# Sums of the down weights made on VectorE from tiles already loaded, stored from GpSimd's queue

## The chip, the cores and the metric

The kernel runs on one core of a Trainium2 chip. The metric is the device time of one execution in microseconds (us). An execution is timed apart from the profile; the profile is one execution of its own.

## The reference, cut to what matters

Two sequences (512 and 1024 tokens of width 1024, float32) each pass through one layer: a mixer (dilated attention beside gated linear attention) and then a feed-forward part. The change touches the feed-forward part alone:

```python
def swiglu(hn, w_gate, w_up, w_down):
    return (jax.nn.silu(hn @ w_gate) * (hn @ w_up)) @ w_down
x = x + swiglu(rmsnorm(x, norm2_g[l]), w_gate[l], w_up[l], w_down[l])
return rmsnorm(x, final_norm_g)
```

`w_gate` and `w_up` are 1024 x 2816, `w_down` is 2816 x 1024.

## The kernel before, in words

The mixer comes first and is not touched. The feed-forward part then takes the 1536 tokens in two blocks of 768 (`NT` = 6 tiles of 128 tokens). Within a block it goes through 11 groups (`NG`) of 2 x 128 columns of `w_gate` and `w_up`, and 2 x 128 rows of `w_down`.

Every product is made of float32 operands that are split in a high part (ScalarE copy, L96) and a low part (VectorE subtraction, L97), and takes three passes of TensorE. The products with `w_gate` and `w_up` go by a scheme of seven products of half-size matrices in place of eight (Strassen in Winograd's form). On the weights' side it needs, of the four quarters of a weight matrix, four sums named 1 to 4; on the tokens' side the forms b11, m2, b21, t3, m1, t4, b22. A product of one form is 12 matmuls of 384 columns (L1116).

- **First block.** The raw quarters of `w_gate` and `w_up` are loaded by SyncE (SP) into tiles `wr` (six buffers, L1032, one 256 KB transfer each, L1065). VectorE makes the sums (`summed`, L1069 to L1082, and L1098) and SP stores them to DRAM (L1073, L1100). After each group comes `down` (L1195): `w_down`'s four quarter tiles are loaded (L1061), split (`rows`, L1188), and each token tile takes 12 matmuls of 512 columns into `dn`, which VectorE adds to the accumulator (L1207). It needs no sums of `w_down`.
- **Second block.** The sums are loaded ready-made (L1063, L1061). `w_down` goes by the scheme of seven too, over pairs of groups (`down` at L1216, matmuls at L1228); only the last group is plain.
- **Strips.** The sums of `w_down` that the second block needs are made between DRAM places while the first block runs: `strips` (L66 to L79) lists 32 copies from ScalarE's queue (L73) and 32 accumulating transfers from GpSimd's queue (L74), 352 KB each. The main loop gives them out at an even pace, each tied to the end of a product (L1342 to L1350).
- **Turns.** In groups 3, 5 and 7 of the first block the tokens of the second block are prepared: `rows` (L934) loads two token tiles into `hx` (L937), with a sum of squares on ScalarE (L940) and the power on GpSimd (L91), at products 0 and 3 of `w_gate`; `turn` (L951) then transposes them (L960), makes the forms, splits them into tiles of the pool `wc`, which the split weights use too, and stores them from SP (L968) in pieces of 512 bytes.

Order of the work. The list `units` (L1260 to L1279) holds the products in order. A plan says at which unit which weight is prepared: four products ahead (`AHEAD`, L1260), `rows` of `w_down` at products 3 to 6 of `w_up` (L1304). Loads are taken from the list `wanted` in order, as far ahead as the count `room` (6, L1311) allows; a prepared tile gives its place back (L1102, L1193). From this the framework makes the queues of the engines, in an order of its own near to the program's, with all waits; every engine and every queue works in order. Pools give a buffer out again when all its readers and stores are done. The pool `sm` (four buffers) holds sums 1 and 2 of a weight in the first block, and two intermediate tiles of a turn.

Of the kernel before, what the change touches and what calls it, by code (L numbers as in the profile page):

```python
# [18 lines left out]
P = 128  # L19
# [24 lines left out]
def tile_trunk(ctx: ExitStack, tc: tile.TileContext, a: dict):  # L44
# [12 lines left out]
    quarters, sums, bulk = {}, {}, []  # L57
    for wn in ("w_gate", "w_up"):
        quarters[wn] = {(i, j): a[wn][0][512 * j:512 * j + 512, FH * i:FH * i + FH] for i in range(2) for j in range(2)}
        sums[wn] = {n: dram.tile([NF // 2, P, 512], F32, name=f"{wn}s{n}") for n in (1, 2, 3, 4)}  # L60
    quarters["w_down"] = {
        (i, j): a["w_down"][0][FH * i:FH * i + FH, 512 * j:512 * j + 512] for i in range(2) for j in range(2)
    }
    sums["w_down"] = {n: dram.tile([FH, 512], F32, name=f"w_downs{n}") for n in (1, 2, 3, 4)}

    def strips():  # L66

        sm, qu = sums["w_down"], quarters["w_down"]
        n, step = 8, FH // 8
        out = [[] for _ in range(n + 3)]  # L70
        for c in range(n):
            rows = slice(step * c, step * c + step)
            copy = lambda o, i, r=rows: nc.scalar.dma_start(out=o[r], in_=i[r])  # L73
            add = lambda o, i, r=rows: nc.gpsimd.dma_start(out=o[r], in_=i[r], accum_op=ALU.add, max_dma_last_dim=2048)  # L74
            out[c] += [(copy, sm[x], qu[y]) for x, y in ((1, (0, 0)), (3, (0, 1)), (2, (1, 1)), (4, (1, 0)))]
            out[c + 1] += [(add, sm[1], qu[0, 1]), (add, sm[3], qu[1, 1])]
            out[c + 2] += [(add, sm[2], sm[1])]
            out[c + 3] += [(add, sm[4], sm[2])]
        return [x for y in out for x in y]  # L79
# [820 lines left out]
    if True:  # L900
# [131 lines left out]
        wr_p = pool(left, "wr", 6, side="left")  # L1032
# [3 lines left out]
        e_p = pool(left, "e", 15, side="left")  # L1036
# [8 lines left out]
        RIGHT = ((0, 0), 2, 3, 4, 1, (1, 1), (1, 0))  # L1045

        class Group:
# [7 lines left out]
            def raw(self, wn, x, n=0):  # L1055

                lo = self.grp * P
                own, tag = (sm_p, "sm") if self.blk and n % 3 == 2 else (wr_p, "wr")
                t = own.tile([P, 512], F32, tag=tag, name=f"r{wn}{self.blk}{self.grp}_{n}")
                if wn == "w_down":  # L1060
                    nc.sync.dma_start(out=t, in_=(sums[wn][x] if isinstance(x, int) else quarters[wn][x])[lo:lo + P])  # L1061
                elif isinstance(x, int):
                    nc.sync.dma_start(out=t, in_=sums[wn][x][self.grp])  # L1063
                else:
# [4 lines left out]
            def summed(self, wn, n):  # L1069

                q = lambda i, j: self.r[wn, (i, j)]
                add = lambda o, i0, i1: nc.vector.tensor_tensor(out=o, in0=i0, in1=i1, op=ALU.add)
                put = lambda x: nc.sync.dma_start(out=sums[wn][x][self.grp], in_=self.r[wn, x])  # L1073
                if n == 1:
                    for x in (1, 2):
                        self.r[wn, x] = sm_p.tile([P, 512], F32, tag="sm", name=f"s{x}{wn}{self.grp}")
                    add(self.r[wn, 1], q(1, 0), q(1, 1))
                    add(self.r[wn, 2], self.r[wn, 1], q(0, 0))
                    add(q(1, 0), q(0, 0), q(1, 0))
                    self.r[wn, 3] = q(1, 0)  # L1080
                    for x in (1, 2, 3):
                        put(x)  # L1082

            def prepare(self, wn, n):

                nm = f"c{wn}{self.blk}{self.grp}_{n}"
                x = (RIGHT if wn == "w_down" else LEFT)[n]
                if wn == "w_down":
                    wc = wd_p.tile([P, 2, 512], F32R, tag="wd", name=nm)
                else:  # L1090
                    own, tag = (hx_p, "hx") if n in (2, 5) else (wc_p, "wc")
                    wc = own.tile([P, 2, 512], F32R, tag=tag, name=nm)
                    if not self.blk:
                        self.summed(wn, n)
# [12 lines left out]
            def product(self, wn, n):  # L1107

                x = FORMS[n]
                if n in (0, 1, 3, 4):  # L1110
                    self.ps[n] = gu_p.tile([P, 512], F32, tag="gu", name="gu")[:, 0:H]
                own = {2: 0, 5: 3, 6: 4}.get(n, n)
                ps, wc, (xh, xl) = self.ps[own], self.w.pop((wn, n)), self.b.B[x]
                for k in range(KH):
                    for i, (wp, src) in enumerate(((0, xh), (0, xl), (1, xh))):
                        ins = nc.tensor.matmul(ps, wc[:, wp, k], src[:, k], start=(own == n and k == 0 and i == 0),  # L1116
                                               stop=(k == KH - 1 and i == 2), skip_group_check=True)
                getattr(self, wn)(n, ps)
                return getattr(ins, "ins", ins)
# [50 lines left out]
            def left(self, n):  # L1170

                sub = lambda o, i0, i1: nc.vector.tensor_tensor(out=o, in0=i0, in1=i1, op=ALU.subtract)
                neg = lambda o, i0, i1: nc.vector.scalar_tensor_tensor(
                    out=o, in0=i0, scalar=-1.0, in1=i1, op0=ALU.mult, op1=ALU.subtract
                )
                a11, a12, a21, a22 = [self.e[x] for x in ((0, 0), (1, 0), (0, 1), (1, 1))]
                if n == 1:
                    self.s1, self.s2 = self.tmp("s1"), self.tmp("s2")
                    sub(self.s1, a22, a21)
                    neg(self.s2, self.s1, a11)  # L1180
                elif n == 2:
                    sub(a21, a11, a21)
                elif n == 5:
                    neg(self.s2, self.s2, a12)
                src = a11 if n == 0 else self.s2 if n in (1, 5) else (a21, a22, self.s1)[n - 2] if n < 5 else a12
                self.w["left", n] = self.factor(f"f{n}_", src)

            def rows(self, f, c):  # L1188
# [3 lines left out]
                split(self.wd[f, c][:, 0], self.wd[f, c][:, 1], self.r["w_down", (f, c)])  # L1192
                return 1  # L1193
# [22 lines left out]
        def down(blk, grps, n, q):  # L1216
# [3 lines left out]
            fresh = n in (0, 4, 6)  # L1220
# [4 lines left out]
            for i, g in enumerate(gs):  # L1225
                x, w = g.w["left", n], g.w["w_down", n]
                for m, (xp, wp) in enumerate(((0, 0), (0, 1), (1, 0))):
# [3 lines left out]
                        (1, 1, ALU.subtract), (0, 1, ALU.subtract), (0, 0, ALU.add))[n]  # L1231
# [57 lines left out]
        def plan(i, key, wn, n):  # L1289
            todo.append((i, key, wn, n))  # L1290
            if wn == "rows":
                wanted.append((key, "w_down", n, 0))
            elif key[0]:
# [4 lines left out]
        for i, u in enumerate(units):  # L1298
            if u[0] == "p":
# [4 lines left out]
                if u[2] == "w_up" and groups[u[1]].plain and u[3] > 2:  # L1304
                    plan(i, u[1], "rows", divmod(u[3] - 3, 2))
# [5 lines left out]
        room = 6  # L1311

        def prepare_to(i):
            nonlocal room
            while todo and todo[0][0] <= i:
# [6 lines left out]
                if wn == "rows":  # L1322
                    room += g.rows(*n)
                else:
                    room += g.prepare(wn, n)
                    if wn == "w_down":
                        g.left(n)
# [4 lines left out]
        strip = strips()  # L1332
        total = len(strip)
        for i, u in enumerate(units):
            prepare_to(i)
            if u[0] == "p":
# [3 lines left out]
                ins = groups[key].product(wn, n)  # L1340

                if key[0] == 0 and 0 < key[1] < NG - 1:  # L1342
                    at = 14 * (key[1] - 1) + n + (7 if wn == "w_up" else 0) + 1
                    while strip and (total - len(strip)) * 14 * (NG - 2) < at * total:
                        f, o, x = strip.pop(0)
                        x = f(o, x)
                        tc.add_manual_dep(
                            getattr(x, "ins", x), ins.name,
                            mybir.DependencyInfo(mybir.DependencyClass.Sync, mybir.DependencyReason.DATA), reason="pace",
                        )  # L1350
# [82 lines left out]
```

## Time and profile before

| | |
|---|---|
| median of 3 runs | 1973.4 us (1972.24 to 1973.72) |
| the profiled execution's own time | 1971.95 us |
| its span, from first to last instruction | 1970.2 us |
| TensorE (matmul) busy | 1910.6 us, 97% of the span |
| VectorE busy | 1365.6 us, 69% |
| ScalarE busy | 885.1 us, 45% |
| GpSimd busy | 109.4 us, 6% |
| moved by DMA | 256.55 MB |

In the rows below, PE is TensorE's matmuls, PEld its weight loads, DVE VectorE, ACT ScalarE, POOL GpSimd and SP SyncE; a q behind the name is the engine's instruction queue. L is a line of the kernel before. A tile's name stands as out<-in, with buffer numbers left out. Matmuls overlap each other, so a busy PE can still be behind its best pace; times from start to start tell more. The queue q1 holds SP's transfers, q10 ScalarE's and q0 GpSimd's.

### The profile page before, as it was taken

To read this page: it belongs to the slowest core of one execution; us is meant where nothing else is said; L and a number is where in the kernel's file an instruction comes from. 1 tells how busy PE (TensorE), PEld (TensorE's weight loads), DVE (VectorE), ACT (ScalarE), POOL (GpSimd) and SP (SyncE) were. 2 spreads that over 40 slices of the span, in tenths; PEclk is the share of its full clock that TensorE was granted. 3 is DMA by queue.
4 is the path that set the end of the run, shared out by engine and by line. 5 is a ranking of instruction groups with operands and counts; after the bars stand their busy time and mean duration, and the time that the engine had idled before them with its cause. 6 is when DMAs were issued, how large, how long until landed. Compare 5 with 4: busy or idle time off the path is not lost.

```text
span 1970.2 us, 33156 instructions
## 1 busy us (share of the span) xinstructions
PE 1910.6 (97%) x12122; PEld 1753.8 (89%) x12122; DVE 1365.6 (69%) x3198; ACT 885.1 (45%) x2123; POOL 109.4 (6%) x146
## 2 busy tenths in 40 slices
PE   7999999999999999999999998889999999999997
PEld 7898889899998888999898888879889998999997
DVE  5687766647577677564866867677665968778686
ACT  6665555545445545332333334233344443434343
POOL 1110001111000000000001000000011000000001
PEclk9999999999998999999999999999999999999999
DMA  5232230202302331455665958677667543444341
GB/s 146 59 96 78 61 99 23 66 4 58 98 25 71 92 118 59 150 187 184 216 164 153 252 155 226 160 202 207 173 254 282 148 129 107 139 118 145 108 132 66
DMA packets 257698, 256.55 MB, mean 130 GB/s; under 512 B 23872, under 2 KB 190848, under 8 KB 257536
## 3 DMA queue, kind: packets, MB, share of 16 engines
q1 hardware_dynamic: 245248, 231.38, 37.9%
q0 software_dynamic: 6144, 11.54, 4.0%
q10 hardware_dynamic: 6144, 11.54, 2.0%
q8 instruction: 95, 1.56, 0.3%
q14 instruction: 67, 0.55, 0.1%
HBM read 199.27 MB, written 78.18 MB: 141 GB/s over the span
## 4 chain that ended last, share of the span: by engine, by line
PE 75%; DMA 10%; DVE 8%; ACT 3%; issue 2%; POOL 1%; SPq 1%; POOLq 0%; DVEq 0%; ACTq 0%
PE gu L1116 23%; PE dn L1228 7%; PE acc L110 7%; PE acc L112 6%; PE acc L111 6%; PE sc L328 3%; PE pv L428 3%; PE trp L405 2%; DMA rw_down<-w_down 2%; PE dn L110 2%; PE dn L112 2%; PE dn L111 2%; PE kv L669 2%; PE acco L110 2%; PE acco L111 1%
## 5 line engine op out<-in xcount | busy, mean ns | idle before, releaser
L1228 PE MATMUL dn<-cw_down,f 128*128 128x512 f32 x630 | 148.9, 390 | 0.0
L1123 DVE TENSOR_TENSOR u<-gu,u 128x384 f32<-128x384 f32 x176 | 97.5, 554 | 73.0 <-PE gu L1116 72.9
L1228 PEld LDWEIGHTS dn<-cw_down,f 128*128 128x128 f32 x630 | 117.8, 188 | 22.3
L96 ACT CAST cw_gate<-rw_gate 128x512 fp32r<-128x512 f32 x132 | 81.3, 620 | 106.5 <-PE gu L1116 59.6
L96 ACT CAST cw_up<-rw_up 128x512 fp32r<-128x512 f32 x132 | 81.1, 619 | 93.8 <-PE gu L1116 63.4
L110 PE MATMUL dn<-wd,g 128*128 128x512 f32 x288 | 113.8, 395 | 2.3 <-DVE xa L1207 2.0
L97 DVE TENSOR_TENSOR cw_up<-rw_up,cw_up 128x512 fp32r<-128x512 f32 x132 | 90.9, 693 | 34.1 <-ACT cw_up L96 30.9
L384 ACT ACTIVATE sm<-sm,st 128x256 f32<-128x256 f32 (+1 forms) x160 | 86.7, 543 | 57.6 <-DVE st L378 57.4
L112 PE MATMUL dn<-wd,g 128*128 128x512 f32 x288 | 112.4, 390 | 0.0
L1207 DVE TENSOR_TENSOR xa<-dn,xa 128x512 f32<-128x512 f32 x144 | 95.9, 687 | 23.6 <-PE dn L112 22.3
L111 PE MATMUL dn<-wd,g 128*128 128x512 f32 x288 | 112.2, 390 | 0.0
L97 DVE TENSOR_TENSOR cw_gate<-rw_gate,cw_gate 128x512 fp32r<-128x512 f32 x132 | 90.3, 687 | 14.6 <-ACT cw_gate L96 9.0
L96 ACT CAST wd<-rw_down 128x512 fp32r<-128x512 f32 x48 | 29.8, 621 | 153.1 <-PE dn L112 100.9
L110 PE MATMUL acc<-w_atb,hnh_b 128*128 128x384 f32 x256 | 91.6, 358 | 0.0
L112 PE MATMUL acc<-w_atb,hnl_b 128*128 128x384 f32 x256 | 88.4, 345 | 0.0
L111 PE MATMUL acc<-w_atb,hnh_b 128*128 128x384 f32 x256 | 88.4, 345 | 0.0
L1233 DVE TENSOR_TENSOR xa<-xa,dn 128x512 f32<-128x512 f32 x105 | 71.9, 685 | 13.9 <-PE dn L1228 12.0
L110 PEld LDWEIGHTS dn<-wd,g 128*128 128x128 f32 x288 | 54.1, 188 | 16.3 <-DVE xa L1207 5.7
L96 ACT CAST cw_down<-rw_down 128x512 fp32r<-128x512 f32 x70 | 43.4, 619 | 53.6 <-PE dn L1228 22.4
L112 PEld LDWEIGHTS dn<-wd,g 128*128 128x128 f32 x288 | 54.1, 188 | 11.2 <-DVE g L97 0.3
L111 PEld LDWEIGHTS dn<-wd,g 128*128 128x128 f32 x288 | 54.1, 188 | 10.2
L97 DVE TENSOR_TENSOR wd<-rw_down,wd 128x512 fp32r<-128x512 f32 x48 | 33.1, 689 | 42.8 <-ACT wd L96 42.8
(436 smaller groups left out, 6009.6 us busy)
## 6 DMA issues: line engine op xcount, KB each, us to landing
rw_down<-w_down SPq DMA_DIRECT2D x78, 256.0 KB, 3.1
rw_gate<-w_gate SPq DMA_DIRECT2D x77, 256.0 KB, 3.1
rw_up<-w_up SPq DMA_DIRECT2D x77, 256.0 KB, 3.4
w_downs<-w_down ACTq DMA_DIRECT2D x32, 352.0 KB, 4.6
rw_gate<-w_gates SPq DMA_DIRECT2D x44, 256.0 KB, 2.7
rw_up<-w_ups SPq DMA_DIRECT2D x44, 256.0 KB, 2.9
rw_down<-w_downs SPq DMA_DIRECT2D x40, 256.0 KB, 3.4
wr_ata<-w_in SPq DMA_DIRECT2D x32, 192.0 KB, 2.5
```

The costliest lines, as they stand in the source:

```text
L96: nc.scalar.copy(out=h, in_=src)
L97: nc.vector.tensor_tensor(out=l, in0=src, in1=h.bitcast(F32), op=ALU.subtract)
L110: nc.tensor.matmul(out, xh, wh, start=(k == 0), stop=False)
L111: nc.tensor.matmul(out, xh, wl, start=False, stop=False)
L112: nc.tensor.matmul(out, xl, wh, start=False, stop=(k == n - 1))
L328: nc.tensor.matmul(outs[hd], lhs(x[b:b + 64]), rhs(y[b:b + 64]), start=(n == 0), stop=(n == 2))
L384: nc.scalar.activation(out=sm[:, cs], in_=sm[:, cs], func=AF.Exp, scale=0.125, bias=st[:, NM, pat, hd, i0 + g:i0 + g + 1], accum_out=st[:, ...
L1116: ins = nc.tensor.matmul(ps, wc[:, wp, k], src[:, k], start=(own == n and k == 0 and i == 0), stop=(k == KH - 1 and i == 2), skip_group_ch ...
L1123: add = lambda o, i0: nc.vector.tensor_tensor(out=o, in0=ps, in1=i0, op=ALU.add)
L1207: nc.vector.tensor_tensor(out=acc[i][:, cs], in0=ps, in1=acc[i][:, cs], op=ALU.add)
L1228: nc.tensor.matmul(ps, x[:, xp, ts], w[:, wp], start=(fresh and i == 0 and m == 0), stop=(i + 1 == len(gs) and m == 2), skip_group_check=True)
L1233: nc.vector.tensor_tensor(out=o, in0=o, in1=ps, op=op)
```

## The change

The strips go. In the first block the sums of `w_down` are made in place on VectorE, from the four raw tiles that `rows` has split, by a new step `sums`: sums 1 and 3 at products 5 and 6 of the group's `w_up`, sums 2 and 4 at products 0 and 1 of the next `w_gate`. Until then these tiles keep their buffers, so there are eight raw tiles in place of six, and 12 tiles `e` in place of 15. All sums, those of `w_gate` and `w_up` too, are stored from GpSimd's queue. Sum 4 of `w_gate` and `w_up` is made at preparation 5 in the buffer of sum 2 (it was made at preparation 2 in that of a raw quarter). In the second block the last three products of `w_down` change places, and one factor is made in place.

```diff
-    def strips():
...
-            copy = lambda o, i, r=rows: nc.scalar.dma_start(out=o[r], in_=i[r])
-            add = lambda o, i, r=rows: nc.gpsimd.dma_start(out=o[r], in_=i[r], accum_op=ALU.add, max_dma_last_dim=2048)
...
-        wr_p = pool(left, "wr", 6, side="left")
+        wr_p = pool(left, "wr", 8, side="left")
...
-        e_p = pool(left, "e", 15, side="left")
+        e_p = pool(left, "e", 12, side="left")
...
-        RIGHT = ((0, 0), 2, 3, 4, 1, (1, 1), (1, 0))
+        RIGHT = ((0, 0), 2, 3, 4, (1, 0), 1, (1, 1))
...
-                put = lambda x: nc.sync.dma_start(out=sums[wn][x][self.grp], in_=self.r[wn, x])
...
+            def sum(self, wn, x, o, i0, i1):
+
+                nc.vector.tensor_tensor(out=o, in0=i0, in1=i1, op=ALU.add)
+                self.r[wn, x] = o
+                nc.gpsimd.dma_start(out=sums[wn][x][self.grp], in_=o)
+
+            def summed(self, wn):
+                a11, a21, a22 = [self.r[wn, x] for x in ((0, 0), (1, 0), (1, 1))]
+                s1, s2 = [sm_p.tile([P, 512], F32, tag="sm", name=f"s{x}{wn}{self.grp}") for x in (1, 2)]
+                self.sum(wn, 1, s1, a21, a22)
+                self.sum(wn, 2, s2, s1, a11)
+                self.sum(wn, 3, a21, a11, a21)
...
-                if not self.blk and n == 2:
-                    a12 = self.r[wn, (0, 1)]
-                    nc.vector.tensor_tensor(out=a12, in0=a12, in1=self.r[wn, 2], op=ALU.add)
-                    self.r[wn, 4] = a12
-                    nc.sync.dma_start(out=sums[wn][4][self.grp], in_=a12)
+                if not self.blk and n == 5:
+                    self.sum(wn, 4, self.r[wn, 2], self.r[wn, 2], self.r[wn, (0, 1)])
...
-                return int(n in (1, 3, 5, 6)) if not self.blk else int(self.blk and n % 3 != 2)
+                return (0, 1, 0, 1, 0, 2, 0)[n] if not self.blk else int(n % 3 != 2)
...
                 split(self.wd[f, c][:, 0], self.wd[f, c][:, 1], self.r["w_down", (f, c)])
+                return int(self.blk)
+
+            def sums(self, x):
+
+                b11, b12, b21, b22 = [self.r["w_down", y] for y in ((0, 0), (0, 1), (1, 0), (1, 1))]
+                o, i = {1: (b11, b12), 3: (b12, b22), 2: (b22, b11), 4: (b21, b22)}[x]
+                self.sum("w_down", x, o, o, i)
                 return 1
...
-            fresh = n in (0, 4, 6)
+            fresh = n in (0, 4, 5)
...
+                if wn == "w_up" and key[0] == 0 and n in (5, 6):
+                    plan(i, key, "sums", 1 if n == 5 else 3)
+                if key[0] == 0 and key[1] and wn == "w_gate" and n < 2 or key == (1, 0) and wn == "w_gate" and n < 2:
+                    plan(i, (0, key[1] - 1 if key[0] == 0 else NG - 1), "sums", 2 if n == 0 else 4)
...
-        room = 6
+        room = 8
...
-                ins = groups[key].product(wn, n)
-
-                if key[0] == 0 and 0 < key[1] < NG - 1:
-                    at = 14 * (key[1] - 1) + n + (7 if wn == "w_up" else 0) + 1
-                    while strip and (total - len(strip)) * 14 * (NG - 2) < at * total:
-                        f, o, x = strip.pop(0)
-                        x = f(o, x)
-                        tc.add_manual_dep(
...
+                groups[key].product(wn, n)
```

## Rows read from the trace of the kernel before

**Rows 1.** Windows: first block, second block; us, busy by engine, clock, DMA share, GB/s
```profile
920.66:1477.82 557.16, 527.55 (x2692) 481.39 (x2690) 396.27 (x677) 198.37 (x372) 38.27 (x45) 0.98 0.70 201
1477.82:1970.20 492.38, 481.14 (x2550) 452.56 (x2548) 364.95 (x636) 209.81 (x400) 15.14 (x16) 0.99 0.44 137
```
**Rows 2.** Chain of waits, second block: start, us, what
```profile
1539.73 4.09 PE dn L1228 x18
1543.83 2.08 PE gu L1116 x12
```
**Rows 3.** Windows: group 2, then groups 3+4, 5+6, 7+8 of the first block
```profile
1001.19:1048.35 47.16, 46.05 (x241) 42.63 (x241) 33.47 (x57) 14.62 (x27) 2.56 (x3) 1.00 0.62 168
1048.35:1149.96 101.61, 96.44 (x497) 88.04 (x497) 74.81 (x128) 36.41 (x68) 7.52 (x9) 0.98 0.72 195
1149.96:1258.63 108.67, 99.87 (x497) 91.06 (x497) 75.13 (x128) 36.49 (x68) 7.49 (x9) 0.95 0.67 192
1258.63:1368.09 109.46, 98.97 (x497) 89.44 (x497) 74.76 (x128) 37.03 (x69) 6.66 (x8) 0.97 0.70 191
```
**Rows 4.** Waits of PE, 920 to 1487: us in total, times, longest
```profile
PE gu L1116 <- ACT u L1126: 9.5, 4, 4.4
PE gu L1116 <- ACT cw_gate L96: 6.8, 4, 2.9
PE gu L1116 <- DVE cw_gate L97: 4.3, 4, 1.3
PE gu L1116 <- DVE u L1123: 4.2, 6, 1.1
```
**Rows 5.** Chain of waits, first block: transfers in it; start, us from issue to landing
```profile
1093.49 8.03 DMA m1l_d<-fm
...
1137.91 4.32 DMA rw_down<-w_down
1148.70 6.22 DMA hx<-x2d_b
...
1257.37 7.93 DMA hx<-x2d_b
```
**Rows 6.** Waits of ACT, 1048.35 to 1368.09: us in total, times, longest
```profile
ACT wd L96 <- DMA rw_down<-w_down: 24.3, 11, 4.0
...
ACT ft L96 <- DMA b22l_d<-fb: 12.4, 3, 4.7
...
ACT cw_up L96 <- DMA t4l_d<-ft: 8.0, 3, 4.4
```
**Rows 7.** DMA, first block: packets, MB, share of 16 engines; issues: KB, us to landing
```profile
q1 hardware_dynamic: 93509, 88.21, 48.4%
q0 software_dynamic: 6144, 11.54, 14.0%
q10 hardware_dynamic: 6144, 11.54, 6.9%
...
w_downs<-w_downs POOLq DMA_DIRECT2D x16, 352.0 KB, 5.9
...
w_gates<-s1w_gate SPq DMA_DIRECT2D x11, 256.0 KB, 2.7
```
**Rows 8.** DMA queues, 1080 to 1116 (the turn of group 3): packets, MB, share
```profile
q1 hardware_dynamic: 10792, 6.89, 64.6%
q0 software_dynamic: 576, 1.08, 20.3%
q10 hardware_dynamic: 384, 0.72, 6.5%
```
**Rows 9.** Landing of the six `hx` loads: min, median, max
```profile
DMA to landing us min/median/max: 3.5/4.2/7.9
```
**Rows 10.** Timeline, DVE and POOL in the turn of group 3: start, us
```profile
1088.81 0.68 DVE L1072 TENSOR_TENSOR s2w_gate<-s1w_gate,rw_gate 128x512 f32<-128x512 f32 x1
1089.40 0.55 DVE L1161 TENSOR_TENSOR e<-e,gu 128x384 f32<-128x384 f32 x1
...
1089.48 0.85 POOL L74 DMA_DIRECT2D w_downs<-w_down  x1 [6.17 <-PE gu L1116]
```

More of the change, by code (lines that the diff above doesn't have):

```diff
@@ L56, in tile_trunk @@
     FH = FF // 2
-    quarters, sums, bulk = {}, {}, []
-    for wn in ("w_gate", "w_up"):
-        quarters[wn] = {(i, j): a[wn][0][512 * j:512 * j + 512, FH * i:FH * i + FH] for i in range(2) for j in range(2)}
-        sums[wn] = {n: dram.tile([NF // 2, P, 512], F32, name=f"{wn}s{n}") for n in (1, 2, 3, 4)}
[L61 to L64, printed above, removed]
-    def strips():
[L68 to L72, printed above, removed]
-            copy = lambda o, i, r=rows: nc.scalar.dma_start(out=o[r], in_=i[r])
-            add = lambda o, i, r=rows: nc.gpsimd.dma_start(out=o[r], in_=i[r], accum_op=ALU.add, max_dma_last_dim=2048)
[L75 to L79, printed above, removed]
+    quarters, sums = {}, {}
+    for wn in ("w_gate", "w_up", "w_down"):
+        if wn == "w_down":
+            part = lambda i, j: a[wn][0][FH * i:FH * i + FH, 512 * j:512 * j + 512]
+        else:
+            part = lambda i, j: a[wn][0][512 * j:512 * j + 512, FH * i:FH * i + FH]
+        quarters[wn] = {(i, j): part(i, j) for i in range(2) for j in range(2)}
+        sums[wn] = {n: dram.tile([NF // 2, P, 512], F32, name=f"{wn}s{n}") for n in (1, 2, 3, 4)}
     cst = ctx.enter_context(tc.tile_pool(name="cst", bufs=1))
@@ L1059, in raw @@
                 t = own.tile([P, 512], F32, tag=tag, name=f"r{wn}{self.blk}{self.grp}_{n}")
-                if wn == "w_down":
-                    nc.sync.dma_start(out=t, in_=(sums[wn][x] if isinstance(x, int) else quarters[wn][x])[lo:lo + P])
-                elif isinstance(x, int):
+                if isinstance(x, int):
                     nc.sync.dma_start(out=t, in_=sums[wn][x][self.grp])
+                elif wn == "w_down":
+                    nc.sync.dma_start(out=t, in_=quarters[wn][x][lo:lo + P])
                 else:
@@ L1115, in product @@
                     for i, (wp, src) in enumerate(((0, xh), (0, xl), (1, xh))):
-                        ins = nc.tensor.matmul(ps, wc[:, wp, k], src[:, k], start=(own == n and k == 0 and i == 0),
-                                               stop=(k == KH - 1 and i == 2), skip_group_check=True)
+                        nc.tensor.matmul(ps, wc[:, wp, k], src[:, k], start=(own == n and k == 0 and i == 0),
+                                         stop=(k == KH - 1 and i == 2), skip_group_check=True)
                 getattr(self, wn)(n, ps)
-                return getattr(ins, "ins", ins)
             def common(self, n, ps):
@@ L1292, in plan @@
                 wanted.append((key, "w_down", n, 0))
+            elif wn == "sums":
+                pass
             elif key[0]:
@@ L1323, in prepare_to @@
                     room += g.rows(*n)
+                elif wn == "sums":
+                    room += g.sums(n)
                 else:
@@ L1331, in tile_trunk @@
         spare = []
-        strip = strips()
-        total = len(strip)
         for i, u in enumerate(units):
```

37 lines of the change are left out of this document (11 added, 26 removed).

## The prediction

> **What bounds the kernel now.** I read the windows by stage first. The edit acts from 920.66, where the first block's products begin, to 1477.82, where the second block's begin; the mixer ahead of it keeps its code. In the second block [rows 1] the chain of waits is TensorE alone: a product takes 2.08 us from start to start, and 18 matmuls of `w_down` take 4.09 us, one behind the other without a gap [rows 2]. That gives TensorE's own pace, and so the floor of the first block: 11 groups of 14 products and 72 `w_down` matmuls, 11 x (14 x 2.08 + 72 x 4.09 / 18) = 11 x 45.48 = 500.3 us. The block takes 557.2 [rows 1]. So 56.9 us are lost there, and nothing that the edit does can bring much more than that.
>
> The windows by group say where. Group 2 loses 47.16 - 45.48 = 1.7 us. The pairs of groups 3+4, 5+6 and 7+8 have a floor of 90.96 each and lose 10.7, 17.7 and 18.5 [rows 3]: 46.9 of the 56.9, in the pairs that hold the turns (their 16 transposes each are in these figures and stay). Part of it is the clock: the mean grants of 0.98, 0.95 and 0.97 [rows 3] are mixtures of the full level (2.4 GHz) and the half one (1.2 GHz), and 2% of 101.6, 5% of 108.7 and 3% of 109.5 are 10.7 us.
>
> Then the waits. TensorE waits 9.5 us in four waits for the copy at L1126, 11.1 for split weights (L96, L97), and 4.2 in six waits for the addition at L1123 [rows 4]. The chain of waits shows what stands behind them: transfers. A store of a turn's form took 8.03 us to land, a load of `w_down` 4.32, loads of `hx` 6.22 and 7.93 [rows 5]. On ScalarE the same names return: 24.3 us for late `w_down` tiles, 12.4 and 8.0 for the turns' stores, whose buffers the next splits need [rows 6]. ScalarE and VectorE work in order, so one late tile holds up the copies and additions behind it, and these are what TensorE waits for.
>
> Last, what makes transfers slow. Over the first block the DMA engines are busy 0.70 of the time [rows 1]; the strips (queues q0 and q10) are 14.0 + 6.9 points of that [rows 7]. In the turn of group 3 they are 20.3 + 6.5 = 26.8 points beside 64.6 for everything of SP [rows 8]: with 91.4 points, the engines are full.
>
> **The change, part by part.**
>
> *Strips removed, turns.* From the 46.9 us I take the clock (10.7), the waits for L1126 (9.5) and half of those for L1123 (2.1); 24.6 are left for the three turns. The strips' 26.8 points go. New are four stores of `w_down` sums a group, 1.05 MB; at SP's rate in that window, 64.6 / 6.89 = 9.4 points for a MB, they cost 9.8. So 17 of 91.4 points are freed. The gain lies between 0 (SP's own 64.6 points hold the turn's stores back anyway) and 24.6. I take 10, under the middle, since two thirds of the traffic stay.
>
> *Strips removed, `hx`.* The two slow `hx` loads took 6.22 and 7.93 us, the median of six is 4.2 [rows 5, 9]. At the median they save 2.0 + 3.7 = 5.7 us of the 9.5; the bounds are 0 and 9.5. ScalarE also loses 32 issues that were tied to the end of a product.
>
> *Eight raw tiles.* Counting the loops out: before, the last three `w_down` tiles of a group are loaded one product ahead of their split, which is 2.08 us for a transfer that took 4.32 [rows 5]. With eight places, four of them kept by `w_down`, they are loaded two or three products ahead, 4.2 to 6.2 us. ScalarE's 24.3 us in 11 waits are 2.2 each [rows 6], about what one more product covers. VectorE's addition is then no longer behind a late split, and of TensorE's 4.2 us [rows 4] I take 4. The other quarters keep five products or more.
>
> *Clock.* It falls to the half level behind TensorE's long waits. If half of these go, I take 6 of the 10.7; bounds 0 and 10.7.
>
> *Sums on VectorE, a cost.* 44 additions; one is followed by the next after 0.59 us [rows 10], 26 us in all. VectorE is busy 396.3 of 557.2 [rows 1], and would be at 422 of some 535, 79%. While the `down` matmuls run this is covered: there VectorE mostly waits for TensorE. In the turns it isn't: there VectorE ran from one instruction to the next [rows 10]. Three turns with four additions are 12 x 0.59 = 7.1 us at most, 0 at best; I take 3.
>
> *Stores moved to GpSimd's queue.* SP loses 88 stores, each behind a wait for VectorE that held up the loads behind it; GpSimd gets 132 at 0.85 us each [rows 10], 112 us beside 557, and loses 32 strips. Behind a store that waits for VectorE stand the other stores and the six powers of `rows`. I put this at 0; at worst each power comes one issue later, 6 x 0.85 = 5 us.
>
> *Other edits.* Sum 2 keeps its buffer until preparation 6 in place of 2. With a turn's two tiles the four buffers of `sm` are full, and the next two sums are wanted five products later, 10.4 us; a store issued and landed takes 0.85 + 5.9 [rows 7, 10]. So 0. In the second block 12 tiles `e` are enough: eight factors, two sums s1 and two of the next group. Its order of products changes, their number doesn't: 0.
>
> Sum: 10 + 5.7 + 4 + 6 - 3 = 22.7 us. The profiled execution's own time is 1971.95 (span 1970.2), so 1949.3. The median of the runs, 1973.4, lies 1.45 above that execution, which gives 1950.7; I say 1950.
>
> **The rivals.**
>
> *VectorE takes over.* The turns stay as slow, now because VectorE can't keep up. For it: in the turns it ran without a gap, and the edit adds four instructions to each. Against: over a pair it is busy 75 of 102 to 109 us [rows 3], and matmuls of `down` can be drawn ahead. Then the turns give 0, the clock 3, the additions cost their 7.1: 5.7 + 4 + 3 - 7.1 = 5.6, so 1973.4 - 5.6 = about 1968; with the turns giving a few us, 1962. I say 1965.
>
> *Slower: buffers held by stores that land late.* The buffer of sum 1 is given back at product 5 of `w_up`, but it is free only when its store has landed; the load that follows in it is needed five or six products on, 10.4 us at least. Issue 0.85, a store of GpSimd at 5.9 and a load at 4.32 make 11.1 [rows 5, 7, 10], already over. It decides from a store landing of 5.2 us on. At 8.03, the longest of rows 5, the load is 2.8 us late in each of 11 groups, 31 us, and in order on SP it holds up all behind it; with 8 us of gain left that is 1973.4 + 31 - 8 = 1996. Against: the 5.9 is that of an accumulating transfer of 352 KB between DRAM places, whereas a 256 KB store of a sum from SP took 2.7 [rows 7]; with 2.7 the sum is 7.9, and nothing is late. The Trainium skill has a rule that speaks for this rival (SBUF — State Buffer, section "SBUF: two separate sides"): a DMA from GpSimd's queue has its descriptors written by GpSimd's cores, and these are locked out of a port shared with VectorE while that runs an operation in a two-port mode, so that the stores would come late. In this trace GpSimd's issue took 0.85 us while VectorE ran additions back to back [rows 10], which shows no such lock; by the rule the time would be this rival's 1996, by the row the forecast's.
>
> *No change.* The strips filled gaps and TensorE's waits have other causes (SP's 64.6 points alone). Then the leads give 4, the additions take about that, and it stays at 1973.
>
> **How the numbers follow.** A measurement here can tell about 0.2% from no change, 3.9 us. The forecast has 0.62, VectorE's rival 0.17, the slow one 0.13, no change 0.08. Low end: turns 20, `hx` 8, lead 4, clock 9, additions 0 make 41, so 1932. High end: VectorE's rival at its upper end, 1968, and some more for a store in front of the powers: 1970. Above lie the slow rival and half of no change. Faster by over 0.2% takes the forecast, and VectorE's rival but for 0.01: 0.78. Slower takes its rival and 0.01 of no change: 0.14. The rest, 0.08, is the same.
>
> **What would show it.** In the profile after: queue q10 without data and q0 with some 132 stores; the landing of the turns' stores and of `hx` nearer 4 us than 8; no row of ScalarE waiting for `w_down` above a few us in all; the mean clock of the pairs at 0.99 or more; the first block at some 534 us, the rest unchanged. I am wrong if the chain of waits in the turns runs through VectorE with TensorE as late as before (VectorE's rival), or through loads that wait for GpSimd's stores (the slow rival); or if the second block differs from its 492.4 us, which I take as fixed.

## The result and the profile after

The changed kernel takes 1951.97 us (median of four runs, 1947.5 to 1954.92) against 1973.12 for the kernel before, a ratio of 0.9891 with a 95% interval of 0.9868 to 0.9914: faster by 1.1%. The profiled execution took 1947.5 us, its span 1945.7.

The windows of the first and of the second block in the kernel after (columns as in [rows 1]):

```profile
918.86:1453.32 534.46, 516.44 (x2691) 472.71 (x2690) 420.24 (x721) 202.11 (x372) 82.00 (x145) 1.00 0.56 185
1453.32:1945.70 492.38, 481.09 (x2550) 452.61 (x2548) 364.25 (x636) 209.34 (x400) 15.13 (x16) 0.99 0.44 140
```

Against [rows 1] the first block is 22.7 us shorter, VectorE is busy 24.0 us longer in it, the DMA engines 0.56 of the time in place of 0.70, and the second block takes the same 492.38 us. The remaining 1.8 us of the span lie in the mixer, which the edit doesn't touch; over the fourteen profiled executions of before, after and the twelve experiments it took 918.9 to 926.5 us. So below a kernel is read by its whole time for the verdict, and by the window of its first block for the place.

Windows of the first group and of the three pairs of [rows 3], after:

```profile
918.86:953.86 35.00, 30.94 (x171) 28.81 (x170) 27.03 (x48) 17.39 (x31) 6.68 (x12) 1.00 0.84 293
...
1046.01:1144.64 98.63, 95.37 (x497) 86.43 (x497) 79.06 (x135) 37.65 (x69) 14.45 (x26) 1.00 0.54 175
1144.64:1244.06 99.42, 95.35 (x497) 86.52 (x497) 79.01 (x135) 37.42 (x69) 14.44 (x26) 1.00 0.55 174
1244.06:1343.70 99.64, 95.39 (x497) 86.44 (x497) 79.01 (x135) 37.29 (x69) 14.80 (x27) 1.00 0.57 180
```

The pairs lose 7.7, 8.5 and 8.7 us against their floor of 90.96, together 24.8 in place of 46.9: 22.1 of the 22.7 us come from there. The granted clock is 1.00, so the 10.7 us of half level are back as far as the rounded grants tell. The other 11.4 are waits. TensorE's waits after, from 918.86 to 1480, which as in [rows 4] takes in some of the second block (total, times, longest):

```profile
PE gu L1096 <- ACT u L1105: 8.0, 5, 2.5
PE gu L1096 <- DVE u L1102: 6.3, 7, 2.2
PE gu L1096 <- DVE cw_gate L82: 1.9, 5, 0.8
...
PE gu L1096 <- ACT cw_up L81: 1.1, 2, 0.6
```

L1096, L1105, L1102, L81 and L82 are the old L1116, L1126, L1123, L96 and L97. The waits for split weights, 11.1 us in [rows 4], are nearly gone; those for the copy have shrunk only from 9.5 to 8.0 (1.1 us of either lie in the second block), and those for VectorE's addition have grown from 4.2 to 6.3. On ScalarE, in the three pairs:

```profile
ACT junk L925 <- DMA hx<-x2d_b: 12.3, 6, 4.0
...
ACT ft L81 <- DMA b22l_d<-fb: 3.1, 3, 1.1
...
ACT wd L81 <- DMA rw_down<-w_down: 2.6, 3, 1.0
```

Late `w_down` tiles went from 24.3 to 2.6 and the turn's stores from 12.4 to 3.1 [rows 6]; what is left is `hx`. The DMA view of the first block has no q10 any more:

```profile
q1 hardware_dynamic: 79826, 63.74, 38.8%
q0 software_dynamic: 10560, 34.61, 17.2%
...
w_downs<-rw_down POOLq DMA_DIRECT2D x44, 256.0 KB, 3.8
...
hx<-x2d_b SPq DMA_DIRECT2D x6, 512.0 KB, 5.5
```

And the chain of waits shows the same shape in each pair, with two other places outside of them (start, us, what):

```profile
921.72 6.85 DMA w_gates<-s2w_gate
...
932.52 5.76 DMA w_ups<-s2w_up
...
1044.41 5.58 DMA hx<-x2d_b
...
1060.73 3.46 DMA hx<-x2d_b
1064.29 1.16 ACT junk L925 x2
...
1143.85 4.93 DMA hx<-x2d_b
...
1378.65 3.99 DMA w_downs<-rw_down
1382.66 4.25 DMA rw_up<-w_up
```

A pair begins with a load of `hx` for which ScalarE's square, in order, holds up the copies behind it. In the first group VectorE waits for the store of sum 2 to land, since sum 4 is written over it in the same buffer:

```profile
938.38 0.69 DVE L1056 TENSOR_TENSOR s2w_up<-s2w_up,rw_up 128x512 f32<-128x512 f32 x1 [3.41 <-DMA w_ups<-s2w_up]
```

The group took 35.00 us in place of 32.79 before. At 1378.65 a load waits for GpSimd's store of a `w_down` sum: the slow rival's mechanism, in small.

### The profile page after: what moved, and what is told of

Its sections match the earlier page's. It is cut to its first block, busy times and chain, and to the rows that moved or that the text cites. A ratio compares the mean times of both kernels' runs of the same rounds, so it can differ in the third digit from the quotient of the medians.

```text
span 1945.7 us, 33284 instructions
## 1 busy us (share of the span) xinstructions
PE 1899.2 (98%) x12122; PEld 1745.2 (90%) x12122; DVE 1388.4 (71%) x3242; ACT 887.6 (46%) x2123; POOL 153.0 (8%) x246
## 4 chain that ended last, share of the span: by engine, by line
PE 77%; issue 7%; DVE 6%; DMA 5%; ACT 2%; POOL 2%; SPq 0%; POOLq 0%; DVEq 0%; ACTq 0%
PE gu L1096 24%; PE dn L1213 7%; PE acc L95 7%; PE acc L97 6%; PE acc L96 6%; PE sc L313 4%; PE pv L413 3%; PE trp L390 3%; PE acco L95 2%; PE acco L96 2%; PE acco L97 2%; PE dn L95 2%; PE dn L97 2%; PE dn L96 2%; PE kv L654 2%
## 5 line engine op out<-in xcount | busy, mean ns | idle before, releaser
L1102 DVE TENSOR_TENSOR u<-gu,u 128x384 f32<-128x384 f32 x176 | 97.5, 554 | 61.2 <-PE gu L1096 60.6
L81 ACT CAST cw_gate<-rw_gate 128x512 fp32r<-128x512 f32 x121 | 74.6, 620 | 134.2 <-PE gu L1096 90.3
L96 PE MATMUL dn<-wd,g 128*128 128x512 f32 x288 | 112.3, 390 | 0.0
L97 PE MATMUL dn<-wd,g 128*128 128x512 f32 x288 | 112.3, 390 | 0.0
L81 ACT CAST cw_up<-rw_up 128x512 fp32r<-128x512 f32 x121 | 74.2, 619 | 77.6 <-PE gu L1096 51.2
L82 DVE TENSOR_TENSOR cw_up<-rw_up,cw_up 128x512 fp32r<-128x512 f32 x121 | 83.1, 691 | 25.9 <-ACT cw_up L81 23.8
L82 DVE TENSOR_TENSOR cw_gate<-rw_gate,cw_gate 128x512 fp32r<-128x512 f32 x121 | 83.1, 688 | 14.3 <-ACT cw_gate L81 6.7
L97 PE MATMUL acc<-w_atb,hnl_b 128*128 128x384 f32 x256 | 88.1, 344 | 0.0
L96 PE MATMUL acc<-w_atb,hnh_b 128*128 128x384 f32 x256 | 88.1, 344 | 0.0
L81 ACT CAST wd<-rw_down 128x512 fp32r<-128x512 f32 x48 | 29.9, 622 | 112.3 <-PE dn L97 102.5
L81 ACT CAST cw_down<-rw_down 128x512 fp32r<-128x512 f32 x70 | 43.0, 619 | 61.1 <-PE dn L1213 40.9
L97 PEld LDWEIGHTS dn<-wd,g 128*128 128x128 f32 x288 | 54.1, 188 | 11.0
L96 PEld LDWEIGHTS dn<-wd,g 128*128 128x128 f32 x288 | 54.1, 188 | 10.5
L390 PE MATMUL trp<-ident,sm 128*128 128x128 f32 x384 | 61.8, 286 | 0.8 <-ACT ptt L395 0.3
```

The costliest lines, as they stand in the source:

```text
L81: nc.scalar.copy(out=h, in_=src)
L82: nc.vector.tensor_tensor(out=l, in0=src, in1=h.bitcast(F32), op=ALU.subtract)
L96: nc.tensor.matmul(out, xh, wl, start=False, stop=False)
L97: nc.tensor.matmul(out, xl, wh, start=False, stop=(k == n - 1))
L390: nc.tensor.transpose(tr[:, i], sm[:, i * P:(i + 1) * P], ident)
L1102: add = lambda o, i0: nc.vector.tensor_tensor(out=o, in0=ps, in1=i0, op=ALU.add)
```

## The experiments

The theory after the result: the strips' traffic was the cost, the additions and GpSimd's stores give a part back, and `hx` is what still stops TensorE. The rivals: the eight raw tiles did it; the queue that stores is of no account; the additions cost nothing; the strips would do no harm now. All twelve runs (ratio to the kernel before on the same chip, with 95% interval; the first block is from the profiled execution; before 557.16, after 534.46):

| run | what | median us | ratio | first block us |
|---|---|---|---|---|
| e1_no_strips | before, strips left out | 1945.16 | 0.9847 [0.9824, 0.9870] | 525.09 |
| e2_eight_tiles | before, eight raw tiles | 1964.64 | 0.9947 [0.9928, 0.9965] | 547.61 |
| e3_sp_stores | after, sums stored from SP | 1946.5 | 0.9856 [0.9831, 0.9880] | 526.65 |
| e4_no_adds | after, 44 additions left out | 1946.87 | 0.9849 [0.9825, 0.9872] | 529.50 |
| a0_changed_again | after, unchanged | 1956.47 | 0.9899 [0.9881, 0.9917] | 538.47 |
| e5_late_norm | after, norm later in the program | 1950.99 | 0.9876 [0.9858, 0.9894] | 533.87 |
| e6_strips_back | after, with the old strips | 2010.88 | 1.0187 [1.0163, 1.0211] | 598.36 |
| e7_five_sum_tiles | after, five buffers for sums | 1952.9 | 0.9884 [0.9868, 0.9901] | 532.84 |
| e8_gpsimd_adds | after, additions on GpSimd, stores on SP | 1965.64 | 0.9940 [0.9922, 0.9957] | 547.03 |
| e9_tied_norm | after, norm tied to a later product | 1945.08 | 0.9841 [0.9826, 0.9856] | 527.29 |
| e10_sp_tied | e9 with sums stored from SP | 1939.8 | 0.9815 [0.9800, 0.9831] | 523.13 |
| e11_down_gpsimd | after, only `w_down` sums from GpSimd | 1949.64 | 0.9860 [0.9844, 0.9877] | 533.34 |

The second run of the unchanged kernel, a0, says how far two profiles of one program lie apart: 534.5 and 538.5 us for the first block. A difference of four us between single profiles says little here; the ratios carry the verdicts. The runs stand in three sets, on three chips (e1 to e4; a0 and e5 to e7; e8 to e11), so a ratio of one set and one of another are compared by way of the kernel before.

**e1: the strips alone.** Edit of the kernel before; the second block then loads quarters of `w_down` where it loaded their sums.

```
-        strip = strips()
-        total = len(strip)
+        strip = []
+        total = 0
...
-  in_=(sums[wn][x] if isinstance(x, int) else quarters[wn][x])[lo:lo + P])
+  in_=quarters[wn][divmod(x - 1, 2) if isinstance(x, int) else x][lo:lo + P])
```

> The kernel before without the strips: the sums of the down weights are not made, and the second block loads quarters in their place (so part of the second block's product is left out of its proper form; the number of loads and products stays). My theory, that the strips' traffic held back the turns' stores and the loads: most of the 21 us gained by the change appear here, 1955 us or less, the turns' stores land in 3 to 5 us in place of 6 to 8, and the granted clock of the three pairs is back at 1.00. Rival, that the longer lead of the loads (eight raw tiles) made the gain: 1965 us or more here.

The window of its first block:

```profile
926.49:1451.58 525.09, 514.75 (x2691) 472.74 (x2690) 395.90 (x677) 199.13 (x372) 10.37 (x13) 1.00 0.53 169
```

32.1 us less than [rows 1], with the old buffers, no addition on VectorE and SP's own stores: 30 us by the ratio (1976.31 x 0.0153). That is more than the change brought, so its other parts cost. TensorE's waits for split weights, 11.1 us in [rows 4], are all but gone with the strips alone:

```profile
PE gu L1116 <- ACT cw_up L96: 1.2, 1, 1.2
PE gu L1116 <- DVE cw_gate L97: 0.8, 1, 0.8
```

But ScalarE keeps most of its waits for late `w_down` tiles. Over the whole first block, in the kernel before and in this run:

```profile
ACT wd L96 <- DMA rw_down<-w_down: 43.8, 19, 4.0
```

```profile
ACT wd L96 <- DMA rw_down<-w_down: 30.8, 18, 3.6
```

So the waits of that kind (24.3 of the 43.8 us lie in the pairs [rows 6]) were not by themselves what stopped TensorE: with 30.8 us of them left, the first block is 25 us above its floor, and TensorE's own waits come to some 10.

One rival is left open. With the strips' traffic go the 32 issues in ScalarE's queue, 0.50 us each and tied to ends of products, and the 32 in GpSimd's. That transfers land sooner speaks for the traffic (the turns' stores of `ft`: 3.3 us in place of 5.5, medians), but no run takes out one without the other.

**e2: eight raw tiles alone.** Edit of the kernel before: the pool of raw tiles and the planner's room 6 to 8, `e` 15 to 12, and the second block's left factor made in place, so that 12 are enough.

```
-        wr_p = pool(left, "wr", 6, side="left")
+        wr_p = pool(left, "wr", 8, side="left")
-        e_p = pool(left, "e", 15, side="left")
+        e_p = pool(left, "e", 12, side="left")
-        room = 6
+        room = 8
```

> The kernel before with eight raw tiles, and the factor of the second block made in place so that 12 tiles e are enough; strips and stores as before. My theory (term of 4 us): ScalarE's 24 us of waits for late down weights fall under 5, TensorE's waits for the addition fall, and the time falls by about 4 us, to 1969. Rival, that the lead made most of the change's gain: 1960 or less. Rival, that transfers only start earlier into full DMA engines: 1973.

A gain of 10.5 us by the ratio (1976.31 x 0.0053), 9.6 by the window, beside the strips. ScalarE's wait for `w_down` over the first block falls from 43.8 to 15.5 us, and in the pairs from 24.3 to 11.0, not under the 5 that I expected. TensorE's waits don't follow: for the copy of a split weight it waits longer than before, 15.0 us in place of 6.8.

```profile
ACT wd L96 <- DMA rw_down<-w_down: 15.5, 6, 3.4
```

```profile
PE gu L1116 <- ACT cw_gate L96: 15.0, 6, 4.8
```

All of TensorE's waits together are 27.5 us in place of 29.1, so they don't hold the gain. TensorE is busy 8.0 us less in the block (519.52 against 527.55), and over groups 5 and 6 the granted clock is 1.00 in place of 0.95: a good part of the gain shows as the clock. Whether lead and strips simply add isn't shown: no run has both without the change's costs. The windows allow it: 32.1 + 9.6, less 5 to 9 for the additions (e4) and 8 to 12 for the queue (e3), leave 21 to 29, and the change brought 22.7 (18.7 in a0).

**e3: the queue.** One line of the changed kernel.

```
-                nc.gpsimd.dma_start(out=sums[wn][x][self.grp], in_=o)
+                nc.sync.dma_start(out=sums[wn][x][self.grp], in_=o)
```

> The changed kernel with all stores of sums from SyncE's queue in place of GpSimd's. My prediction priced the move of the queue at 0: then 1952 here, within 4 us. Rival: SyncE's stores wait for VectorE's sums and hold up the loads behind them, so that this run is slower by 5 us or more. Rival the other way: GpSimd's stores land later, and this run is faster by 4 us or more, by earlier buffers.

Faster than the changed kernel: 0.9856 against a0's 0.9899, intervals that just don't touch (0.9880, 0.9881), some 8 us; with the first comparison of the changed kernel, 0.9891 [0.9868, 0.9914], they do. The trace goes the same way. TensorE's and VectorE's waits in its first block:

```profile
PE gu L1096 <- DVE u L1102: 1.3, 2, 1.1
```

```profile
DVE s1w_gate L1056 <- DMA rw_gate<-w_gate: 3.4, 2, 1.9
...
DVE s1w_up L1056 <- DMA rw_up<-w_up: 2.3, 4, 1.0
```

and VectorE's in the changed kernel:

```profile
DVE s1w_up L1056 <- DMA rw_up<-w_up: 7.5, 6, 2.4
...
DVE s2w_up L1056 <- DMA w_ups<-s2w_up: 5.6, 3, 3.4
...
DVE s2w_gate L1056 <- DMA w_gates<-s2w_gate: 3.6, 1, 3.6
```

With the sums stored from SP, VectorE no longer waits for a sum's store of `w_up` to land or as long for loads of `w_up`, and TensorE waits 1.3 us for VectorE's addition in place of 6.3. The gain isn't spread evenly. Windows of the first group and of the three pairs together, in this run:

```profile
922.98:960.78 37.80, 32.69 (x170) 30.98 (x169) 29.71 (x51) 17.42 (x31) 0.00 (x0) 0.91 0.85 284
1053.70:1341.89 288.19, 282.25 (x1490) 260.34 (x1489) 237.39 (x407) 112.72 (x206) 4.23 (x6) 1.00 0.58 182
```

The pairs take 9.5 us less than the changed kernel's 297.69, but the first group takes 2.8 us more than its 35.00. There the store of sum 2 of `w_gate`, which sum 4 overwrites, stands in SP's queue behind loads and lands later still, and TensorE waits 4.3 us for that weight. From the chain of waits:

```profile
930.51 9.83 DMA w_gates<-s2w_gate
```

The other runs agree: the first group took 37.6 to 38.2 us wherever the sums of `w_gate` and `w_up` are stored from SP (e3, e8, e10, e11), and 34.2 to 35.0 where they are stored from GpSimd. No run stores the first group's sums from one queue and the rest from the other.

**e11: which stores.** Gate and up sums from SP, those of `w_down` from GpSimd.

```
+                (nc.gpsimd if wn == "w_down" else nc.sync).dma_start(out=sums[wn][x][self.grp], in_=o)
```

> The changed kernel with the stores of the gate and up sums from SyncE's queue, and those of the down sums alone from GpSimd's. If GpSimd's queue costs by the down tiles held for a landing (SyncE waits 81 us for such landings), this is as slow as the changed kernel, 0.990 and 534 to 538. If it costs because sums stored from a second queue share the DMA engines with the turn's stores at once, this is as fast as the run with SyncE's stores, 0.986 and 527.

The ratio is that of e3, the first block that of the changed kernel. VectorE's wait for stores of `s2w_up` is gone here too, TensorE's for the addition is 4.9 in 7. The first group and the pairs:

```profile
918.85:956.44 37.59, 32.64 (x170) 30.93 (x169) 29.82 (x52) 17.45 (x31) 1.82 (x3) 0.91 0.85 285
1050.06:1343.19 293.13, 284.45 (x1489) 261.71 (x1489) 237.05 (x406) 112.67 (x205) 17.41 (x30) 0.99 0.57 179
```

So the first block is as long as the changed kernel's for two reasons that nearly cancel: the first group is as slow as in e3, and the pairs lie between e3's 288.19 and the changed kernel's 297.69 (302.12 in a0). The ratio puts the cost on the stores of `w_gate` and `w_up`, the pairs of this one profile on both kinds; which of the stores costs, and how much, stays open.

**e4: the additions.** The store keeps its place, the sum isn't made.

```
-                self.sum("w_down", x, o, o, i)
+                self.r["w_down", x] = o
+                nc.gpsimd.dma_start(out=sums["w_down"][x][self.grp], in_=o)
```

> The changed kernel without the 44 additions for the down weights: the raw quarters are stored in their place, so the sums are left out. My prediction priced the additions at 3 us: 1949 here. Rival, that VectorE bounds the turns: 1945 or less (7 us at most by 12 additions in the turns, 0.59 each). If they are wholly covered: 1952.

0.5 points below a0, with separate intervals: 9.9 us (1975 x 0.005); by the windows 5 to 9. VectorE is busy 22 us less in the first block (397.99 against 420.24), so a quarter to nearly a half of what it is spared comes off the end. A part of that may be the stores: without the sum a store waits only for its raw tile and no longer for VectorE, which this run doesn't separate.

**e6: the strips beside the changed kernel.** The old list of transfers, from the weights into scratch places, with the old pacing.

```
+    scratch = {n: dram.tile([FH, 512], F32, name=f"scratch{n}") for n in (1, 2, 3, 4)}
...
+                    while strip and (total - len(strip)) * 14 * (NG - 2) < at * total:
+                        f, o, x = strip.pop(0)
+                        x = f(o, x)
...
```

> The changed kernel with the old strips run beside it once more, into a place that nothing reads. If the traffic itself is the price (32 us in the first block, by the kernel before without strips), this loses 20 us or more, a first block of 555 or more, with the turns' stores landing in 6 to 8 us again. Rival, that the strips cost the kernel before so much only because its loads came one product ahead: 10 us or less here.

1.0187 against 0.9899: 57 us, nearly twice the 30 to 32 that they cost in the kernel before. The window of the first block, and TensorE's waits in it:

```profile
924.64:1523.00 598.36, 536.42 (x2691) 491.92 (x2690) 422.75 (x721) 202.49 (x372) 113.38 (x177) 0.95 0.69 204
```

```profile
PE gu L1113 <- ACT u L1123: 24.3, 4, 10.4
PE gu L1113 <- DVE u L1120: 22.1, 10, 7.3
```

The clock is 0.95 over the block (0.98 in the kernel before), ScalarE waits 25.8 us for `hx`, whose loads land in 6.7 us (median) in place of 5.5, and TensorE waits behind both engines. The turns' stores did not come back to the 6 to 8 us that I expected: their medians are 3.9 to 4.6, the longest 8.7. The 32 accumulating strips stand in GpSimd's queue among the 132 stores here, so that traffic and queue can't be told apart in the 57 us; together with e1 it does show that strips of this size cost tens of us in either kernel.

**e5 and e9: the square that waits for `hx`.** The split of `rows` into a load and a norm, the norm three products later. In e5 only the order in the program was changed (norm at products 2 and 6 of `w_gate`).

> The changed kernel with the sum of squares of the two token tiles of a turn taken out of the place right behind their loads: at products 2 and 6 of the gate weights, in place of 0 and 3. My theory on what is left: ScalarE works in order and stands still until the load of a token tile has landed (12.3 us in six waits), and TensorE then waits for the copy behind it, 1.9, 2.0 and 2.7 us in the three turn groups: 6 us less here, a first block of 528. Rival, that the waits move to the turn's transposes, which then come later: no gain.

The square was put ahead of the copies all the same: ScalarE waits 15.2 us in six waits for `hx`, TensorE 7.8 for the copy, and the interval of 0.9876 overlaps a0's. The aim was not reached, so this decides nothing. e9 ties the square to the end of product 3 or 6:

```
+                if after is not None:
+                    tc.add_manual_dep(getattr(sq, "ins", sq), after.name, ...)
...
+                    if wn == "w_gate" and n in (3, 6):
+                        blocks[1].norm(2 * q + n // 6, ins)
```

> The changed kernel with the sums of squares of a turn's two token tiles tied to the end of products 3 and 6 of the gate weights, so that the framework can't put them ahead again, as it did in the run before with the same aim. Theory: the stalls of TensorE of 2 to 4 us behind these loads in the three turn groups go, 6 us less: a ratio of 0.986, a first block of 529 to 532. Rival: the turn's transposes come too late in their place, and nothing is gained.

TensorE's waits in its first block:

```profile
PE gu L1106 <- DVE u L1113: 7.7, 12, 1.5
PE gu L1106 <- DVE cw_gate L82: 1.4, 4, 0.8
PE gu L1106 <- ACT u L1116: 1.0, 1, 1.0
```

The waits for the copy, 6.9 us in the changed kernel's first block and 8.4 in a0's, are 1.0, ScalarE waits 2.6 us for `hx` in place of 12.3, and the ratio falls from 0.9899 to 0.9841 with separate intervals (below the first comparison's 0.9868 too): 11.5 us (1975 x 0.0058); 7 to 11 by the windows. The load itself still takes 5.0 us. So what stopped TensorE was where the square stood on ScalarE, and the transfer's length matters only through that.

**e10: both.** e9 with the line of e3.

> Stores from SyncE's queue and the tied sums of squares together, as a candidate that beats both kernels: if the two gains are independent (8 and 5 us), 1939 or so on a chip where the kernel before takes 1975, a ratio of 0.982, a first block of 521.

1939.8 us, 0.9815: faster than both kernels, with an interval below a0's and the first comparison's, and the lowest first block. It touches e9's, so the queue's share is again only likely (0.26 points, 5 us). The pattern of e3 returns: against e9 the first group is 3.9 us longer (38.23 against 34.33), the pairs together 8.2 us shorter (282.47 against 290.69).

**e7: five buffers for sums** (`sm` 4 to 5, `e` 12 to 11), since the first group waits for sum stores.

> The changed kernel with five buffers for sums in place of four (and 11 tiles e in place of 12, to make room). My prediction said that sum 2, kept to preparation 6 while its store lands, costs 0: then no change here. Rival: VectorE stands still for buffers whose stores from GpSimd are late (3.6 and 5.6 us of waits on stores of sum 2), and this run gains 4 us or more in the first block, most of it in group 0.

0.9884, inside a0's interval. VectorE's wait for the stores of `s2w_up` is still 5.5 us in three. No effect shown, and none could be on that wait: sum 4 is written over sum 2 in its own tile, which a fifth buffer doesn't free. So this run doesn't decide what the wait costs.

**e8: the additions on GpSimd**, stores from SP.

```
-                nc.vector.tensor_tensor(out=o, in0=i0, in1=i1, op=ALU.add)
+                (nc.gpsimd if wn == "w_down" else nc.vector).tensor_tensor(out=o, in0=i0, in1=i1, op=ALU.add)
...
-                nc.gpsimd.dma_start(out=sums[wn][x][self.grp], in_=o)
+                nc.sync.dma_start(out=sums[wn][x][self.grp], in_=o)
```

> The changed kernel with all stores of sums from SyncE's queue, and the 44 additions for the down weights on GpSimd in place of VectorE (a 128x512 product there took 1.30 us, an addition may take as long: 57 us of an idle engine). If the additions' price is VectorE's time, this run adds the 5 us of the run without additions to the gain of the run with SyncE's stores: 1942 or less, a ratio of 0.983, a first block of 522. Rival, that their price is the buffers held for their stores: as the run with SyncE's stores, 0.9856 and 527, or slower by the later stores.

Slower than with the additions on VectorE (e3) by 0.84 points, 17 us, with separate intervals. Groups of the first block here (count, total us, mean ns, idle before):

```profile
L1056 POOL TENSOR_TENSOR rw_down<-rw_down,rw_down 128x512 f32<-128x512 f32 x44 | 63.1, 1434 | 411.2 <-DVE wd L82 281.9 <-DVE rw_gate L1056 62.8 <-DMA rw_down<-w_down 43.9
...
L82 DVE TENSOR_TENSOR wd<-rw_down,wd 128x512 fp32r<-128x512 f32 x44 | 43.5, 1001 | 6.4 <-ACT wd L81 6.4
```

and the last of them in a0, where VectorE makes the additions:

```profile
L82 DVE TENSOR_TENSOR wd<-rw_down,wd 128x512 fp32r<-128x512 f32 x44 | 29.9, 685 | 5.0 <-ACT wd L81 5.0
```

GpSimd takes 1434 ns for an addition, and VectorE's own instructions beside it grow, so VectorE's busy time rises to 427.96 us although 44 instructions left it. SP waits too, with stores in line behind GpSimd's sums; what of the 17 us is which isn't told apart:

```profile
SPq L1058 <- POOL rw_down L1056: 111.8, 24, 17.4
```

## Why the prediction was right, and which of its terms were not

The forecast's time (1950), its sign, its place (the pairs, the second block unchanged) and the first block of some 534 us came out. The sum of 22.7 us did, but by errors that cancel: strips and tiles were priced too low, additions, stores and sum 2 too low as costs. So the closeness of the figure, within 2 us of 1950, is luck; the place and the sign are not. By the steps:

- **Strips, 21.7 us with `hx` and clock: too small.** e1 gives 30 to 32. The clock gave back its 10.7 us, where I took 6: the grants of the three pairs are 1.00 (0.99 over the pairs in a0). The 11.1 us of waits for split weights, from which I took nothing for the strips, went with them (2.0 in e1). For the turns I took 10; their stores of `fm` landed in 2.6 us in place of 6.5 and of `ft` in 3.4 in place of 5.5 (medians), as said, but those of `fb` in 4.5 in place of 3.2.
- **`hx`, 5.7 us: wrong in its mechanism.** I let the two slow loads fall to the median of 4.2 us [rows 9] and took the difference from TensorE's wait. The loads now take 4.9 to 5.6 us, all six alike, and TensorE still waits 8.0 us for the copy: 1.5 less than before. Even without strips (e1) the median is 4.9. The step that failed took the transfer's length as the cost; e9 shows that it was the place of the waiting square ahead of the copies on ScalarE.
- **Eight raw tiles, 4 us: right in kind, 10 beside the strips (e2), but unproved without them.** ScalarE's waits went, as said; TensorE's for VectorE's addition, from which I took the 4 us, didn't (4.2 to 6.3, and 5.2 in e2). What stands behind the gain in e2 is in good part the clock; TensorE's waits for split weights grew there, from 11.1 to 16.6 us.
- **Additions, cost 3 us: too small.** 5 to 10 (e4); even my bound of 7.1 for the turns alone is below the ratio's 9.9. The cover that I named, VectorE waiting for TensorE during the `down` matmuls, holds for more than half of the 22 us, not for all outside the turns.
- **GpSimd's stores, priced at 0 and at most 5: wrong.** Moving them back gave 5 to 8 us by the ratios of two pairs (e10 against e9, e3 against a0), only the second with separate intervals. My step looked at the powers of `rows` and at SP's relief, not at what has to wait until a store has landed. How the 5 to 8 us come about isn't shown: they arise in the pairs, whereas in the first group, where VectorE's waits for landings are longest, SP's queue is the slower one.
- **Sum 2's buffer, 0: wrong in the first group.** I allowed 10.4 us until the next sum takes the buffer, and overlooked sum 4, which the edit itself writes over sum 2 at preparation 5. In the first group, where no product runs ahead, the store of `s2w_gate` took 6.85 us in the chain of waits, that of `s2w_up` 5.76, VectorE waited 3.6 and 3.4 us for them, and the group took 35.00 us in place of 32.79.

Of the rivals, *VectorE takes over* named the right engine, but the pairs gained 22 us with VectorE busy 79 of 99: it costs without being the bound. *No change* fell with e1. The *slow rival* was to decide from a store landing of 5.2 us on; `w_down` sums landed in 3.8 (median), and it shows at one place of the chain (3.99, then a load of 4.25 behind it). SP's queue of loads stood 97 us in all for such landings, but only this one lies on the chain. A lock on GpSimd's descriptors doesn't show either. GpSimd's issues in the first block (count, total us, mean ns, idle before):

```profile
L1058 POOL DMA_DIRECT2D w_downs<-rw_down x44 | 23.8, 540 | 168.8 <-DVE rw_down L1056 168.8
```

540 ns each, and behind nothing but the additions that make the sums. The rule that I drew on (the Trainium skill, SBUF — State Buffer, section "SBUF: two separate sides") speaks of VectorE's two-port modes; a later section of that page, "Who interferes with whom", says that an operation of two tensors, as these additions are, has no such mode. So I had applied the rule where it doesn't hold.

The gain in one line: about 30 us by the strips, some 10 by the lead beside them, 5 to 10 given back by the additions and some 5 to 8 by the stores' queue. How far the first two overlap isn't measured, so these don't add up to the last us. Left open: whether the strips' traffic or their issues cost, which of the stores cost on GpSimd's queue and how, and why strips cost 57 us in the changed kernel and 30 in the old one.

## What to carry to other kernels

Idle time of ScalarE before a late tile is no measure of what the tile costs: e1 kept 30.8 of 43.8 us of such waits, and its first block is within 2 us of the best one here (e10), while some 13 us before `hx` cost 11 (e9 against a0), because copies that TensorE needed stood in line behind that wait. So ask of each wait on an in-order engine what stands behind it, and move the waiting instruction before you speed up the transfer. And when background traffic is replaced by work on an engine that is 70% busy, its price can be a quarter to nearly a half of its duration, as here (one run, e4), and not only its share in the tightest stretch; try each queue for the new stores. A result that is written over another in place has to wait until the store of the first has landed, so ask how long that store takes where nothing runs ahead.

## What the runs showed of the hardware that I had not expected

GpSimd's additions slow VectorE down. In e8 VectorE's subtraction `wd` took 1001 ns in the mean beside GpSimd's additions and 685 without them, and that of `cw_gate` 813 in place of 686; others, as that of `cw_up`, stayed at 686. The Trainium skill has this rule (SBUF — State Buffer, section "Who interferes with whom"): a VectorE instruction with two inputs in SBUF contends with a GpSimd instruction that reads SBUF. The rows of e8 agree; the size here was 46% on one group and nothing on another.

Transfers that run between DRAM places beside the work are not free filler: strips that took 20.9 points of the DMA engines' time [rows 7] cost, with their issues, 30 us of 557, a part of it through the granted clock (0.95 to 0.98 in the pairs before, 1.00 after, and 0.95 over the block with the strips back in e6).
